# A hybrid GLA and SSD block on one core: own space for the split of h tiles 4 to 7, the scaled x of the SSD state taken from PSUM on VectorE, and the GLA output scaling shared by two engines

## The chip, the core and the metric

The kernel runs on one core of one Trainium2 chip. A core has TensorE (PE, matrix products, results in PSUM), VectorE (DVE), ScalarE (ACT), GpSimd (POOL) and SyncE (SP, which issues most DMAs). The metric is the device time of one execution in microseconds.

## The reference, cut to what matters

One layer on 2048 tokens of width 1024. The input projection feeds two token mixers; their outputs are concatenated, projected, and added to the input; a gated embedding follows.

```python
u = rmsnorm(h, norm_w)
q, k, v, g, gate_lr, z, xbc, dt_raw = split_columns(u @ w_in, SPLIT_SIZES)
# GLA: 4 heads, state 128 x 256
gla_out = rmsnorm(gla_chunked(q, k, v, log_a), gla_norm_w) * silu(g)
# SSD: 2 groups, 16 heads of 64, state 128
xs, bm, cm = split(silu(causal_depthwise_conv(xbc)))
def step(state, inp):                       # per chunk
    y = (cb * decay_ij) @ xdt + (ci @ state) * exp(cum)      # xdt = x * dt
    decay_to_end = exp(cum[-1] - cum)
    state = state * exp(cum[-1]) + bi^T @ (xdt * decay_to_end)
y = rmsnorm((y + xs * d_skip) * silu(z), ssd_norm_w)
h = h + concat(gla_out, y) @ w_out
gate = sigmoid(rmsnorm(h, pe_norm_w) @ w_pe_gate)
h = h + gate * (p_i @ w_pe)
out = rmsnorm(h, final_norm_w)
```

## The kernel before, in words

The tokens are worked on in four blocks of 512 (block 0 to 3), each of four steps of 128 tokens (t = 0 to 3). Activations lie with the channel on the partitions: a tile is 128 channels by 512 tokens. Every large product is made in three matmuls of split operands: each operand is a high half, rounded to the matmul's format, and a low half, the rest; TensorE adds high by high, high by low and low by high into one PSUM bank (`dense_t`, lines 254 to 256). Making the two halves of an activation is one ScalarE instruction for the high half, and one on VectorE or GpSimd for the low half. In block 0 the weights are split on the way (ScalarE L196, VectorE L197) and written back; blocks 1 to 3 load the split weights.

In each block the dense products of the input projection run on TensorE while the GLA heads and the SSD groups are worked on beside them. These side parts are Python generators, stepped in between the dense products; the order on each engine is then set by the framework's scheduler, so an engine's queue mixes instructions of several parts. PSUM has four banks for the dense products (`psd`) and four for the rest (`pss`). Each tile name has a few buffers; a new tile waits until the last reader of the buffer that it takes over is done.

The change touches four places.

The SSD steps (`ssd_steps`, two groups a block, four steps a group, so 32 steps). `make_x` transposes four tiles of x into a bank of PSUM (L602). VectorE multiplies the bank with `dt` to give `xd` (L604). GpSimd multiplies `xd` with `dte`, the decay to the end of the chunk, to give `xe` (L607). ScalarE casts `xe` to the high half of `xh` (L611), GpSimd makes the low half (L612). `make_m` makes the decay matrices `em` (two a step) from a DMA with ScalarE (L634, L636) and VectorE (L637). In the step proper TensorE makes `ips` (L652), `yps` from `xd` and `em` (L657), and `nps`, the new part of the state, from `xh` (L660 to L662). GpSimd decays the state `sS` (L663), VectorE adds (L665 to L670), where L665 makes `ec`, the part of the output that comes from the old state.

The end of a GLA head (`gla_steps`). The head's output stands in PSUM for four steps. ScalarE scales each step's 128x256 with the reciprocal norm `rs` (written in the profile as `yy`, after the chain L287 to L302 that makes it) to give `on` (L563). TensorE transposes `on` in two halves e2 = 0 and 1 (L569), VectorE multiplies with the gate (L573), ScalarE casts the high half into `mq` (L574) and GpSimd makes the low half (L575). Out-projection matmuls (L878 to L880) then read `mq`.

The h tiles. The last output projection of a block (`out_proj(ht, mqd, h_done)`) adds to the eight tiles of h (VectorE L881), and calls `h_done` for each tile d. This scales by the norm weight and splits: high half on ScalarE (L995), low half on VectorE (L996), squares on ScalarE (L350, L353) added up on GpSimd (L356). Tiles 0 to 3 go into one buffer of `mq`, tiles 4 to 7 into the next. There are two buffers, and one of them is `mqd`, which the projection itself reads until its end. The gate product then reads all eight (L254 to L256 with operand `mq`), and the sum of squares goes through TensorE (L320).

The table of `dte` (L472, L473), made once a block: 128 by four steps by 16 heads.

Of the kernel before, what the change touches and what calls it, by code (L numbers as in the profile page):

```python
# [6 lines left out]
F32 = mybir.dt.float32  # L7
F32R = mybir.dt.float32r
# [3 lines left out]
ALU = mybir.AluOpType  # L12
# [23 lines left out]
def hybrid_kernel(ctx, tc, x_nat, x_t, p_t, w_t, w_n0, w_n, w_o, w_g, w_p, prm, gup, cst, out):  # L36
# [384 lines left out]
    def lr_steps(lrn, lrT, dtr, cx):  # L421
# [51 lines left out]
        act(out=flat(dte), in_=flat(dte), func=AF.Exp)  # L473
        cx.update(dt=dt, cum=cum, elast=elast, dte=dte, cd=cd, ecd=ecd)
# [38 lines left out]
    def gla_steps(h, v, sg, fs, qm, km, mq):  # L513
# [48 lines left out]
        for t in range(NT):  # L562
            act(out=on[:, t, :], in_=rs_in[t // 2][:, (t % 2) * 256:(t % 2 + 1) * 256], func=AF.Copy,  # L563
                scale=rs[:, t:t + 1])
        yield
        for e2 in range(2):
            ps = pss.tile([P, TB], F32, name="pss")
            for t in range(NT):
# [6 lines left out]
            nc.gpsimd.tensor_tensor(out=mq[:, 1, kt, :], in0=og, in1=mq[:, 0, kt, :].bitcast(F32),  # L575
                                    op=ALU.subtract)
# [3 lines left out]
    def ssd_steps(g, bt, ctl, xs, cx):  # L580
# [18 lines left out]
        def make_x(t):  # L599
            xps = pss.tile([P, TB], F32, name="pss")  # L600
            for m in range(4):
                nc.tensor.transpose(out=xps[:, m * P:(m + 1) * P], in_=xs[:, m, t * P:(t + 1) * P], identity=ident)  # L602
            xd = sb.tile([P, 8, 64], F32, name="xd", tag="xd", bufs=SB["xd"])
            tt(out=xd, in0=xps.rearrange("p (h c) -> p h c", c=64),  # L604
               in1=dt[:, t, h8].unsqueeze(2).broadcast_to([P, 8, 64]), op=ALU.mult)
            xe = sb.tile([P, 8, 64], F32, name="xe", tag="tmp", bufs=SB["tmp"])
            nc.gpsimd.tensor_tensor(out=xe, in0=xd, in1=dte[:, t, h8].unsqueeze(2).broadcast_to([P, 8, 64]),  # L607
                                    op=ALU.mult)
# [101 lines left out]
    def new_mq():  # L710
        return big.tile([P, 2, 4, TB], F32R, name="mq", tag="mq", bufs=2)
# [41 lines left out]
    for b in range(NB):  # L753
# [232 lines left out]
        hw = [None, None]  # L986
        hsq = SumSq()

        def h_done(d):
            if d % 4 == 0:  # L990
                hw[d // 4] = new_mq()
            hd = ht[:, d, :]
            w = pr[:, C_PW + d:C_PW + d + 1]
            hq = hw[d // 4]
            act(out=hq[:, 0, d % 4, :], in_=hd, func=AF.Copy, scale=w)  # L995
            stt(out=hq[:, 1, d % 4, :], in0=hd, scalar=w, in1=hq[:, 0, d % 4, :].bitcast(F32),  # L996
                op0=ALU.mult, op1=ALU.subtract)
            hsq.add(hd)
# [14 lines left out]
        for d, cs in jobs:  # L1013
# [13 lines left out]
            gps = dense_t(lambda k: hw[k // 4][:, 0, k % 4, cs], lambda k: hw[k // 4][:, 1, k % 4, cs], n, gw[d],  # L1027
# [104 lines left out]
```

## Time and profile before

| | us |
|---|---|
| Runs | 1873.10, 1877.78, 1881.28 |
| Median | 1877.78 |
| The profiled execution | 1877.63 |
| Its span, first to last instruction | 1875.9 |
| TensorE busy | 1831.1 |
| VectorE busy | 1021.3 |
| ScalarE busy | 776.1 |
| GpSimd busy | 383.4 |

The mean granted clock of TensorE was 0.994 of full speed. Busy times are sums over the span; an instruction's time runs from its start to its end, and the ends of matmuls overlap the starts of the next. A wait is idle time of an engine just before an instruction; the profile names what ended it. Lines are those of the kernel before.

### The profile page before, as it was taken

The page shows a single profiled execution, that of the slowest core. Times are in us where ns is not written, and L with a number is a line of the kernel's source. Part 1 is how long each engine was busy: PE and PEld are TensorE (multiplying, and loading weights), DVE is VectorE, ACT ScalarE, POOL GpSimd, SP SyncE. Part 2 cuts the span into 40 slices and gives each one's busy share as a digit, 9 for nine tenths or more (in the row PEclk, how much of TensorE's full clock was granted, in tenths as well). Part 3 has the DMA queues.
Part 4 walks back from the last instruction along what each step waited for, and adds up shares of the span by engine and source line. Part 5 has one row for each costly group of instructions (what it writes and reads, how often), then busy time and mean ns, then how long its engine had stood idle before and what let it go on. Part 6 is the DMA issues. An engine that isn't in the chain of part 4 may idle for free.

```text
span 1875.9 us, 25880 instructions
## 1 busy us (share of the span) xinstructions
PE 1831.1 (98%) x9674; PEld 1538.6 (82%) x9674; DVE 1021.3 (54%) x1959; ACT 776.1 (41%) x1557; POOL 383.4 (20%) x355
## 2 busy tenths in 40 slices
PE   8989999999999999999999999999999999999997
PEld 6878888877887888887788788887888888888887
DVE  8776676477566345425555544523546545551544
ACT  6575454355355334224434533313424453321431
POOL 3132012034203101204311310301420221020222
PEclk9999999999999999999999999999999999999998
DMA  7767686778785557556568556655657755666651
GB/s 271 266 214 268 225 304 217 267 245 286 256 285 162 185 164 235 161 180 214 181 225 251 154 172 197 203 176 176 217 178 264 214 157 169 182 196 187 204 174 46
DMA packets 131853, 390.60 MB, mean 208 GB/s; under 512 B 13712, under 2 KB 32400, under 8 KB 131344
## 3 DMA queue, kind: packets, MB, share of 16 engines
q1 hardware_dynamic: 129744, 382.39, 63.0%
q0 software_dynamic: 1984, 6.55, 0.9%
q8 instruction: 76, 1.25, 0.3%
q14 instruction: 49, 0.40, 0.1%
HBM read 306.58 MB, written 82.31 MB: 207 GB/s over the span
## 4 chain that ended last, share of the span: by engine, by line
PE 76%; DVE 5%; DMA 4%; ACT 3%; issue 2%; POOL 1%; SPq 0%; DVEq 0%; ACTq 0%; POOLq 0%
PE psd L256 14%; PE psd L254 14%; PE psd L255 14%; PE psd L880 5%; PE psd L879 5%; PE psd L878 5%; PE psd L277 3%; PE psd L275 3%; PE psd L279 3%; PE pss L558 1%; PE pss L657 1%; PE pss L554 1%; DMA xp<-x_t 1%; PE pss L652 1%; DMA wkl<-wk_t 1%
## 5 line engine op out<-in xcount | busy, mean ns | idle before, releaser
L254 PE MATMUL psd<-u,wkl 128*128 128x512 f32 x864 | 343.0, 397 | 0.2
L255 PE MATMUL psd<-u,wkl 128*128 128x512 f32 x864 | 337.6, 391 | 0.0
L256 PE MATMUL psd<-u,wkl 128*128 128x512 f32 x864 | 337.2, 390 | 0.0
L254 PEld LDWEIGHTS psd<-u,wkl 128*128 128x128 f32 x864 | 162.3, 188 | 34.9 <-issue 1.9
L256 PEld LDWEIGHTS psd<-u,wkl 128*128 128x128 f32 x864 | 162.2, 188 | 34.1
L255 PEld LDWEIGHTS psd<-u,wkl 128*128 128x128 f32 x864 | 162.6, 188 | 32.5 <-issue 0.7
L356 POOL TENSOR_TENSOR sq<-sq,sqt 128x512 f32<-128x512 f32 (+1 forms) x77 | 98.7, 1282 | 396.5 <-ACT sqt L353 396.5
L879 PE MATMUL psd<-mq,wkl 128*128 128x512 f32 x384 | 151.5, 395 | 1.8 <-POOL mq L575 1.7
L878 PE MATMUL psd<-mq,wkl 128*128 128x512 f32 x384 | 153.2, 400 | 0.0
L412 DVE SCALAR_TENSOR_TENSOR acc<-psd,hcw,acc 128x511 f32<-128x511 f32 x144 | 107.1, 744 | 79.7 <-ACT acc L409 77.8
L880 PE MATMUL psd<-mq,wkl 128*128 128x512 f32 x384 | 150.0, 391 | 0.0
L197 DVE TENSOR_TENSOR whl<-wraw,whl 128x512 fp32r<-128x512 f32 (+1 forms) x136 | 110.1, 816 | 52.9 <-ACT whl L196 52.7
L881 DVE TENSOR_TENSOR ht<-ht,psd 128x512 f32<-128x512 f32 x128 | 87.3, 684 | 93.9 <-PE psd L880 93.2
L634 ACT ACTIVATE em<-em,cum 128x128 f32<-128x128 f32 x256 | 83.3, 391 | 105.2 <-DMA em<-cd 99.6
L196 ACT CAST whl<-wraw 128x512 fp32r<-128x512 f32 (+1 forms) x136 | 82.2, 618 | 72.2 <-PE psd L256 26.9
L275 PE MATMUL psd<-wkl,u 128*128 128x256 f32 (+1 forms) x384 | 111.5, 290 | 0.0
L277 PE MATMUL psd<-wkl,u 128*128 128x256 f32 (+1 forms) x384 | 109.8, 286 | 0.0
L279 PE MATMUL psd<-wkl,u 128*128 128x256 f32 (+1 forms) x384 | 109.7, 286 | 0.0
L254 PE MATMUL psd<-u,whl 128*128 128x512 f32 x272 | 108.9, 400 | 0.0
L255 PE MATMUL psd<-u,whl 128*128 128x512 f32 x272 | 107.6, 396 | 0.7 <-DVE u L389 0.4
L256 PE MATMUL psd<-u,whl 128*128 128x512 f32 x272 | 107.3, 395 | 0.3 <-DVE whl L197 0.3
L575 POOL TENSOR_TENSOR mq<-sg,mq 128x512 fp32r<-128x512 f32 x32 | 43.7, 1370 | 278.5 <-ACT mq L574 278.5
(282 smaller groups left out, 3940.0 us busy)
## 6 DMA issues: line engine op xcount, KB each, us to landing
wkl<-wk_t SPq DMA_DIRECT2D x216, 512.0 KB, 4.1
wkl<-wk_o SPq DMA_DIRECT2D x96, 512.0 KB, 3.6
wk_t<-whl SPq DMA_DIRECT2D x72, 512.0 KB, 3.7
wkl<-wk_g SPq DMA_DIRECT2D x44, 512.0 KB, 3.6
wraw<-w_t SPq DMA_DIRECT2D x36, 512.0 KB, 5.0
wkl<-wk_n SPq DMA_DIRECT2D x36, 512.0 KB, 3.6
em<-cd SPq DMA_DIRECT2D x64, 256.0 KB, 4.2
wk_o<-whl SPq DMA_DIRECT2D x32, 512.0 KB, 3.6
```

The costliest lines, as they stand in the source:

```text
L197: tt(out=t[:, 1, :], in0=s, in1=t[:, 0, :].bitcast(F32), op=ALU.subtract)
L254: mm(out=ps, lhsT=hi[:, sl], rhs=rhi(k), start=(k == 0), stop=False)
L255: mm(out=ps, lhsT=hi[:, sl], rhs=rlo(k), start=False, stop=False)
L256: mm(out=ps, lhsT=lo[:, sl], rhs=rhi(k), start=False, stop=(k == KT - 1))
L275: mm(out=outs[t], lhsT=ug(0, k)[:, ts], rhs=hi[:, sl], start=first, stop=False, skip_group_check=True)
L277: mm(out=outs[t], lhsT=ug(0, k)[:, ts], rhs=lo[:, sl], start=False, stop=False, skip_group_check=True)
L279: mm(out=outs[t], lhsT=ug(1, k)[:, ts], rhs=hi[:, sl], start=False, stop=last, skip_group_check=True)
L356: self.eng.tensor_tensor(out=self.acc[:, cs], in0=self.acc[:, cs], in1=sq, op=ALU.add)
L412: stt(out=acc[:, s:TB], in0=ps[:, 0:TB - s], scalar=w(j), in1=acc[:, s:TB], op0=ALU.mult, op1=ALU.add)
L878: mm(out=ps, lhsT=hi[:, sl], rhs=mq[:, 0, k, :], start=(k == 0), stop=False)
L879: mm(out=ps, lhsT=hi[:, sl], rhs=mq[:, 1, k, :], start=False, stop=False)
L880: mm(out=ps, lhsT=lo[:, sl], rhs=mq[:, 0, k, :], start=False, stop=(k == 3))
```

## The change

1. `dte` is multiplied by `dt` once a block, on VectorE.
2. In `make_x`, `xe` is made on VectorE from the PSUM bank with that product, ahead of `xd`; GpSimd has no part in it any more.
3. Of the four scalings of a GLA head's output the first two stay on ScalarE, the last two go to VectorE. Of the two low halves the second (e2 = 1) goes from GpSimd to VectorE.
4. Tiles 0 to 3 of h are split into a buffer of `mq` as before. Tiles 4 and 5 get a new tile `hx` in space of the name `xs`, tiles 6 and 7 get four tiles `hs` in spaces of `bt`, `ctl`, `cb` and `ec`, all names of the SSD part.

```diff
         act(out=flat(dte), in_=flat(dte), func=AF.Exp)
+        tt(out=dte, in0=dte, in1=dt, op=ALU.mult)
...
         for t in range(NT):
-            act(out=on[:, t, :], in_=rs_in[t // 2][:, (t % 2) * 256:(t % 2 + 1) * 256], func=AF.Copy,
-                scale=rs[:, t:t + 1])
+            o = rs_in[t // 2][:, (t % 2) * 256:(t % 2 + 1) * 256]
+            if t < 2:
+                act(out=on[:, t, :], in_=o, func=AF.Copy, scale=rs[:, t:t + 1])
+            else:
+                nc.vector.tensor_scalar_mul(out=on[:, t, :], in0=o, scalar1=rs[:, t:t + 1])
...
             nc.scalar.copy(out=mq[:, 0, kt, :], in_=og)
-            nc.gpsimd.tensor_tensor(out=mq[:, 1, kt, :], in0=og, in1=mq[:, 0, kt, :].bitcast(F32),
-                                    op=ALU.subtract)
+            eng = nc.vector if e2 else nc.gpsimd
+            eng.tensor_tensor(out=mq[:, 1, kt, :], in0=og, in1=mq[:, 0, kt, :].bitcast(F32), op=ALU.subtract)
...
+            xp3 = xps.rearrange("p (h c) -> p h c", c=64)
+            xe = sb.tile([P, 8, 64], F32, name="xe", tag="tmp", bufs=SB["tmp"])
+            tt(out=xe, in0=xp3, in1=dte[:, t, h8].unsqueeze(2).broadcast_to([P, 8, 64]), op=ALU.mult)
             xd = sb.tile([P, 8, 64], F32, name="xd", tag="xd", bufs=SB["xd"])
-            tt(out=xd, in0=xps.rearrange("p (h c) -> p h c", c=64),
-               in1=dt[:, t, h8].unsqueeze(2).broadcast_to([P, 8, 64]), op=ALU.mult)
-            xe = sb.tile([P, 8, 64], F32, name="xe", tag="tmp", bufs=SB["tmp"])
-            nc.gpsimd.tensor_tensor(out=xe, in0=xd, in1=dte[:, t, h8].unsqueeze(2).broadcast_to([P, 8, 64]),
-                                    op=ALU.mult)
+            tt(out=xd, in0=xp3, in1=dt[:, t, h8].unsqueeze(2).broadcast_to([P, 8, 64]), op=ALU.mult)
...
-        hw = [None, None]
+        hq = [None] * KT
...
+        def h_tiles(d):
+            if d == 0:
+                t = new_mq()
+                for k in range(4):
+                    hq[k] = (t[:, 0, k, :], t[:, 1, k, :])
+            elif d == 4:
+                t = sb.tile([P, 2, 2, TB], F32R, name="hx", tag="xs", bufs=SB["xs"])
+                for k in range(2):
+                    hq[4 + k] = (t[:, 0, k, :], t[:, 1, k, :])
+            elif d >= 6:
+                hq[d] = tuple(sb.tile([P, TB], F32R, name="hs", tag=tag, bufs=SB[tag])
+                              for tag in (("bt", "ctl"), ("cb", "ec"))[d - 6])
+
         def h_done(d):
-            if d % 4 == 0:
-                hw[d // 4] = new_mq()
+            h_tiles(d)
...
-            act(out=hq[:, 0, d % 4, :], in_=hd, func=AF.Copy, scale=w)
-            stt(out=hq[:, 1, d % 4, :], in0=hd, scalar=w, in1=hq[:, 0, d % 4, :].bitcast(F32),
-                op0=ALU.mult, op1=ALU.subtract)
+            hi, lo = hq[d]
+            act(out=hi, in_=hd, func=AF.Copy, scale=w)
+            stt(out=lo, in0=hd, scalar=w, in1=hi.bitcast(F32), op0=ALU.mult, op1=ALU.subtract)
```

The order on the engines changes with it. The first place is step t = 2 of the first SSD group in block 1, on TensorE. Before:

```order
L652 MATMUL pss<-ctl,sS_112 128x128 x4
L256 MATMUL psd<-u,wkl 128x512
L657 MATMUL pss<-em,xd 64x128 x3
L509 MATMUL pss<-v,kn 128x256
L510 MATMUL pss<-v,kn 128x256
L511 MATMUL pss<-v,kn 128x256
L657 MATMUL pss<-em,xd 64x128 x5
L254 MATMUL psd<-u,wkl 128x512
L660 MATMUL pss<-xh,bn 128x512
L255 MATMUL psd<-u,wkl 128x512
L661 MATMUL pss<-xh,bn 128x512
L662 MATMUL pss<-xh,bn 128x512
```

After, where the lines of the same code are three higher in this part (one higher in the GLA part):

```order
L256 MATMUL psd<-u,wkl 128x512
L254 MATMUL psd<-u,wkl 128x512
L255 MATMUL psd<-u,wkl 128x512
L256 MATMUL psd<-u,wkl 128x512
L660 MATMUL pss<-em,xd 64x128 x3
L510 MATMUL pss<-v,kn 128x256
L511 MATMUL pss<-v,kn 128x256
L512 MATMUL pss<-v,kn 128x256
L660 MATMUL pss<-em,xd 64x128 x5
L663 MATMUL pss<-xh,bn 128x512
L664 MATMUL pss<-xh,bn 128x512
L665 MATMUL pss<-xh,bn 128x512
```

A group of three dense matmuls (L254 to L256) has moved in front of the `em` matmuls (L657, now L660), and the three matmuls with `xh` (L660 to L662, now L663 to L665) stand together.

The same step on ScalarE, from the cast of the step before it to the cast of `xh` for this step. Before:

```order
L611 CAST xh<-xe 128x512
L636 ACTIVATE em<-em 128x512
L634 ACTIVATE em<-em,cum 128x128
L523 CAST amh<-am 128x512
L634 ACTIVATE em<-em,cum 128x128 x3
L543 ACTIVATE km<-gT_104,fs 128x256
L636 ACTIVATE em<-em 128x512
L634 ACTIVATE em<-em,cum 128x128 x5
L636 ACTIVATE em<-em 128x512
L611 CAST xh<-xe 128x512
```

After (`em` is L637 and L639 there, the cast L614):

```order
L614 CAST xh<-xe 128x512
L637 ACTIVATE em<-em,cum 128x128 x2
L524 CAST amh<-am 128x512
L639 ACTIVATE em<-em 128x512
L637 ACTIVATE em<-em,cum 128x128 x3
L544 ACTIVATE km<-gT_104,fs 128x256
L639 ACTIVATE em<-em 128x512
L637 ACTIVATE em<-em,cum 128x128 x4
L614 CAST xh<-xe 128x512
```

Between the two casts stood three exponentials of `em` (L636) before, and two after (L639).

The second place is the end of the last output projection in block 0, on ScalarE, where the h tiles are split. L196 splits weights, L387 makes the u of the next block. Before:

```order
L995 ACTIVATE mq<-ht,pr 128x512
L353 ACTIVATE sqt<-ht 128x512
L387 CAST u<-xp 128x512
L196 CAST wpe<-wraw 128x512 x2
L353 ACTIVATE sqt<-ht 128x512
L387 CAST u<-xp 128x512
L353 ACTIVATE sqt<-ht 128x512
L196 CAST whl<-wraw 128x512 x2
L353 ACTIVATE sqt<-ht 128x512
L387 CAST u<-xp 128x512
L995 ACTIVATE mq<-ht,pr 128x512 x4
L353 ACTIVATE sqt<-ht 128x512
```

After (the split is L1010):

```order
L353 ACTIVATE sqt<-ht 128x512
L196 CAST wpe<-wraw 128x512 x2
L1010 ACTIVATE hx<-ht,pr 128x512
L353 ACTIVATE sqt<-ht 128x512
L387 CAST u<-xp 128x512
L1010 ACTIVATE hx<-ht,pr 128x512
L353 ACTIVATE sqt<-ht 128x512
L196 CAST whl<-wraw 128x512 x2
L1010 ACTIVATE hs<-ht,pr 128x512
L353 ACTIVATE sqt<-ht 128x512
L387 CAST u<-xp 128x512
L1010 ACTIVATE hs<-ht,pr 128x512
```

The four splits of tiles 4 to 7, which stood together behind the projection, now stand each beside the square (L353) of its own tile.

## Rows read from the trace of the kernel before

**Rows 1.** Busy times and instructions by engine, whole span.

```profile
PE 1831.1 (98%) x9674; PEld 1538.6 (82%) x9674; DVE 1021.3 (54%) x1959; ACT 776.1 (41%) x1557; POOL 383.4 (20%) x355
```

**Rows 2.** TensorE's waits: line waited for, total us, times, longest us.

```profile
PE pss L661 <- POOL xh L612: 2.7, 4, 0.9
...
PE pss L660 <- ACT xh L611: 2.3, 4, 0.7
PE psd L879 <- POOL mq L575: 2.2, 4, 0.6
...
PE psd L254 <- ACT mq L995: 2.1, 1, 2.1
PE pss L660 <- DVE sh L290: 2.0, 1, 2.0
...
PE pss L657 <- DVE em L637: 1.8, 1, 1.8
PE pss L569 <- ACT on L563: 1.8, 3, 0.8
...
PE pss L320 <- POOL sq L356: 0.8, 2, 0.4
```

**Rows 3.** Windows: us; busy of PE, PEld, DVE, ACT, POOL; clock; DMA; GB/s.

```profile
95.00:105.00 10.00, 9.81 (x63) 8.16 (x64) 9.79 (x18) 8.00 (x21) 3.47 (x3) 1.00 0.96 288
111.90:115.30 3.40, 1.94 (x8) 0.98 (x7) 1.40 (x5) 1.97 (x5) 2.67 (x2) 1.00 1.00 276
115.40:118.70 3.30, 3.30 (x10) 2.71 (x11) 1.47 (x4) 1.75 (x5) 0.00 (x0) 0.50 0.85 339
129.10:132.40 3.30, 3.30 (x9) 2.58 (x8) 1.38 (x6) 0.13 (x1) 0.00 (x0) 0.50 0.67 266
```

**Rows 4.** Timeline of TensorE, block 1: start, us, operation, [idle before].

```profile
579.72 0.39 PE L255 MATMUL psd<-u,wkl 128*128 128x512 f32 x1
579.95 0.39 PE L256 MATMUL psd<-u,wkl 128*128 128x512 f32 x1
...
585.95 0.65 PE L657 MATMUL pss<-em,xd 128*64 128x128 f32 x6
...
588.95 0.50 PE L660 MATMUL pss<-xh,bn 128*128 128x512 f32 x1 [0.57 <-ACT xh L611]
...
602.16 0.33 PE L569 MATMUL pss<-cf,on 128*128 128x128 f32 x1 [0.48 <-ACT on L563]
```

**Rows 5.** Lines: busy us, mean ns; idle before, what ended it.

```profile
L604 DVE TENSOR_TENSOR xd<-pss,dt 128x512 f32<-128x512 f32 x32 | 21.9, 685 | 3.7 <-PE pss L602 3.7
...
L607 POOL TENSOR_TENSOR xe<-xd,dte 128x512 f32<-128x512 f32 x32 | 38.0, 1189 | 173.5 <-DVE xd L604 169.6 <-DVE fs L499 3.9
```

**Rows 6.** Timeline of VectorE, block 1, the crowded step.

```profile
584.80 0.69 DVE L604 TENSOR_TENSOR xd<-pss,dt 128x512 f32<-128x512 f32 x1
```

**Rows 7.** Timeline of GpSimd, blocks 0 and 1.

```profile
88.54 2.09 POOL L607 TENSOR_TENSOR xe<-xd,dte 128x512 f32<-128x512 f32 x1 [3.92 <-DVE fs L499]
...
586.87 1.04 POOL L607 TENSOR_TENSOR xe<-xd,dte 128x512 f32<-128x512 f32 x1
```

**Rows 8.** Timeline of TensorE, block 0, the SSD steps.

```profile
115.35 0.80 PE L661 MATMUL pss<-xh,bn 128*128 128x512 f32 x1 [0.85 <-POOL xh L612]
...
127.57 0.47 PE L660 MATMUL pss<-xh,bn 128*128 128x512 f32 x1 [2.04 <-DVE sh L290]
```

**Rows 9.** Timeline of VectorE, block 0, the SSD steps.

```profile
109.57 1.29 DVE L637 TENSOR_TENSOR em<-em,cb 128x512 f32<-128x512 f32 x2
...
121.49 2.13 DVE L637 TENSOR_TENSOR em<-em,cb 128x512 f32<-128x512 f32 x2
...
126.75 0.68 DVE L665 TENSOR_TENSOR ec<-ec,pss 128x512 f32<-128x512 f32 x1
```

**Rows 10.** Timeline of VectorE, block 0, split of the h tiles.

```profile
435.85 4.29 DVE L996 SCALAR_TENSOR_TENSOR mq<-ht,pr,mq 128x512 fp32r<-128x512 f32 x4 [0.71 <-ACT mq L995]
```

**Rows 11.** Timeline of TensorE, block 0, gate product.

```profile
439.65 2.08 PE L320 MATMUL pss<-sq,cf 128*128 128x512 f32 x2
```

More of the change, by code (lines that the diff above doesn't have):

```diff
@@ L985, in hybrid_kernel @@
             side.append(gu)
-        hw = [None, None]
+        hq = [None] * KT
         hsq = SumSq()
+        def h_tiles(d):
[10 more added lines that the diff above has]
+                              for tag in (("bt", "ctl"), ("cb", "ec"))[d - 6])
         def h_done(d):
-            if d % 4 == 0:
-                hw[d // 4] = new_mq()
+            h_tiles(d)
             hd = ht[:, d, :]
             w = pr[:, C_PW + d:C_PW + d + 1]
-            hq = hw[d // 4]
-            act(out=hq[:, 0, d % 4, :], in_=hd, func=AF.Copy, scale=w)
-            stt(out=hq[:, 1, d % 4, :], in0=hd, scalar=w, in1=hq[:, 0, d % 4, :].bitcast(F32),
-                op0=ALU.mult, op1=ALU.subtract)
+            hi, lo = hq[d]
+            act(out=hi, in_=hd, func=AF.Copy, scale=w)
+            stt(out=lo, in0=hd, scalar=w, in1=hi.bitcast(F32), op0=ALU.mult, op1=ALU.subtract)
             hsq.add(hd)
@@ L1026, in hybrid_kernel @@
                 mm(out=pps, lhsT=lo[:, sl], rhs=pb[:, ks], start=False, stop=(k == 1))
-            gps = dense_t(lambda k: hw[k // 4][:, 0, k % 4, cs], lambda k: hw[k // 4][:, 1, k % 4, cs], n, gw[d],
+            gps = dense_t(lambda k: hq[k][0][:, cs], lambda k: hq[k][1][:, cs], n, gw[d],
                           None if yh else h_sum)
```

## The prediction

> **What bounds the kernel now.** I read the busy times first [rows 1]: TensorE is busy 1831.1 us of a span of 1875.9, so at most some 45 us can be had without taking matmuls away, and this change takes none away. VectorE has 54%, ScalarE 41%, GpSimd 20%. So a move between those three counts only where TensorE waits for one of them. Next I read the table of TensorE's waits and kept the rows on lines that the change touches [rows 2]: the split state input `xh` (L660, L661), `em` (L657), the scaled GLA output (L569), the low half of the GLA output (L879) and the split of the h tiles (L254, L320). Then I followed each wait into the timelines, and read the granted clock around those in block 0 [rows 3]. The reader is to see that the waits are few and short. Together the rows of group 2 hold 15.7 us: under 1% of the span.
>
> A wait costs more than its idle time. A dense matmul that took 0.39 us was followed after 0.23 us by the next one [rows 4], so 0.16 us of overlap is lost with each wait.
>
> **The state input, xe from PSUM.** Before, `xd` is made on VectorE (32 of 685 ns), then GpSimd makes `xe` from it (32 of 1189 ns) [rows 5], then ScalarE the high half of `xh`, then GpSimd the low half. After, `xe` is the first VectorE operation on the PSUM tile and `xd` the second. In the crowded step of block 1, `xd` stood at 584.80 and took 0.69, and GpSimd began `xe` only at 586.87, behind other work of its own, and took 1.04 [rows 6, 7]. So `xe` ended at 587.91. With the change it ends at about 585.5: the chain to `xh` can win up to 2.4 us. How much it wins is set by ScalarE, which makes the high half in the order of its queue: the cast for this step moves ahead of one exponential (the order in the part on the change), about half a microsecond; the rest of what stands in front of it stays. TensorE waited there 0.57 us for the high half at 588.95 [rows 4], and for the low half, which GpSimd makes from it, again. In the whole run these are 2.3 + 2.7 us in four places each [rows 2], one in each block, and 8 x 0.16 us of lost overlap: 6.3 us. A whole dense group of three (3 x 0.23 = 0.69 us) also moves in front of the `em` matmuls in the new order of TensorE, which covers more. I take 5.0 of the 6.3 as gone, and leave 0.3 per block for the next late operand, `em` on ScalarE's queue. From the other side: nothing goes (0), or all does (6.3).
>
> In block 0 two more waits belong to this chain. At the first step `em` was 1.8 us late [rows 2]; ScalarE's `xh` cast stood in front of it, behind a GpSimd `xe` that began at 88.54 and took 2.09 [rows 7]. I take 1.0 of the 1.8. Then L660 waited 2.0 us at 127.57 [rows 2, 8]. The row names the tiny `sh`, but its bank was released by `ec`, which ended at 126.75 + 0.68 [rows 9]. `ec` stood behind an `em` pair that took 2.13 us beside GpSimd's `xe`, where the same pair took 1.29 at 109.57 [rows 9]. That saves 0.84, but `xe` itself comes in on VectorE with 0.69. What helps beyond the 0.15 is that the other GpSimd work moves out of the way. I take 1.1 of the 2.0; the ends are 0 and 2.0.
>
> On the difference between the two `em` pairs the Trainium skill has a rule (SBUF — State Buffer, "Who interferes with whom"): a VectorE instruction with two SBUF inputs contends with a GpSimd instruction that reads SBUF, one with at most one SBUF input does not. The two pairs here agree, 2.13 against 1.29 us. By it the new `xe` and `xd`, which read PSUM, never slow down, and 32 slowed neighbours go. The same skill (Perfetto Trace Analysis, "Optimizing Scalar/DVE Operations") warns that moving work between GpSimd and VectorE might not help, since they share a read port. For the PSUM reads the first rule excludes that here; for the low halves of the GLA output, two SBUF inputs, it would hold, and then that edit is worth nothing, as the sum nearly has it.
>
> **The clock.** In block 0 the granted clock was 0.50 in two stretches of 3.3 us in which TensorE was busy all the time; the first came directly behind a stretch in which it was busy 1.94 of 3.40 us, with these very waits in it [rows 3, 8]. At full clock each stretch is half as long: 1.65 us each, 3.3 together. I take all of the first and half of the second, 2.5, because half of the wait ahead of the second remains; ends 0 and 3.3.
>
> **The h split.** Before, tiles 4 to 7 went into the second buffer of `mq`, which is free only when the last output projection has read it, so four high and four low halves came in a bunch: VectorE took 4.29 us for the four lows [rows 10]. The wait at L254 for it is 2.1 us, at block 0 only; blocks 1 and 2 lose 0.8 at the sum of squares L320 [rows 2]. After, each is split as its h tile is made. In block 0 I expect no gain: VectorE has its weight splits and h additions between the lows, so the last low comes hardly sooner, and the sum of squares that L320 takes in at 439.65 [rows 11] still comes through GpSimd's additions. In blocks 1 and 2 the wait on the squares goes: 0.8 + 2 x 0.16 = 1.1. Ends: 0, and with block 0 2.1 + 0.16 more. The new space (`xs`, `bt`, `ctl`, `cb`, `ec`) is free there, since the SSD steps of the block are done; if one were still held, the split would wait as it did before.
>
> **The GLA output.** Of 64 scalings 32 go from ScalarE to VectorE, of 32 low halves 16 go from GpSimd to VectorE. L569 waited 1.8 us [rows 2], but for the *first* `on`, which stays on ScalarE: at 602.16 a single transpose waits [rows 4]. I take 0 (ends 0 and 1.8). L879 waits for the first low half of the last head, which stays on GpSimd: 2.2 in four places [rows 2], of which 0.4 may go because the operations in front come sooner (ends 0 and 2.2).
>
> **What it adds.** VectorE gets 32 x 0.685 = 21.9 us of `xe`, and 32 scalings and 16 low halves, which no row of VectorE shows; by the row of `xd` they are at most 48 x 0.685 = 32.9 us, all beside TensorE's work at the end of a head, where it waits for the first scaling only. Where it has slack this costs nothing: the cover is TensorE's own work. The bank of the transposed x is held some 0.69 us longer, and `xd` is later by as much. In the crowded step `xd` ended at 585.49 and TensorE came to it at 585.95 [rows 4, 6], 0.46 us of slack, so alone it would be 0.23 us late; with the 0.69 us of dense work placed in front, the slack is 0.46 again. Where VectorE is full, 9.79 of 10 us at 95 to 105 [rows 3], some shows. I put +1.0 for all of it (ends 0 and 21.9). The product of `dte` and `dt`, four tiny operations on 128x64, costs nothing: it is done long before the steps.
>
> **Sum.** -5.0 - 1.0 - 1.1 - 2.5 - 1.1 - 0.4 + 1.0 = -10.1 us, against the profiled execution's 1877.63 (1.7 us around its span, 0.15 below the median shown): 1867.5 us.
>
> **Rivals.**
> 1. *The waits only move on.* Of the 6.3 us 2 go, because `em` or `ec` is late instead, the clock dips stay, and the additions cost 1.0: 1876.6, with 1873 to 1879 around it. For it speaks that ScalarE's and VectorE's queues are crowded in just these steps; against it that a group of dense matmuls moved in front. Chance 0.27.
> 2. *All goes.* 6.3 + 1.8 + 2.0 + 2 x 0.16 + 3.3 + 1.1 + 2.3 for block 0's split + 2.2 for L879 = 19.3, with nothing added: 1858.3, or 1854 to 1862. For it speaks that the covers are large in the other steps; against it that block 0's split has a second chain behind it. Chance 0.15.
> 3. *Slower: VectorE becomes the bound of the SSD steps.* `xd` is behind `xe`, and L657 waits for `xd` at each step: up to 32 x 0.685 = 21.9 us, less gains of 11.1 at most: 1888.4. It decides if the slack before L657 is under 0.69 us in most steps; 0.46 in the crowded step and 9.79 of 10 busy speak for it, against it that VectorE was busy only 54% of the span [rows 1] and that three steps in four have dense groups between the transposes and L657. Chance 0.08.
>
> **Numbers.** The forecast has 0.50, with 1862 to 1873 as its own range. No change within 0.5% (9.4 us, about what a measurement of this kernel can tell) is 1868.4 to 1887.2. Of the forecast's 0.50 I put 0.29 below 1868.4; with rival 2 that is 0.44 faster. Rival 1 and the rest of the forecast are 0.48, rival 3 is 0.08. The range 1856 to 1879 leaves out most of rival 3 and the lower end of rival 2.
>
> **What would show it.** Right: `xe` is on VectorE at some 685 ns; the rows L660 and L661 for `xh` (new L663, L664) are gone or below 0.3 us each; the half-clock stretch at 115 us is gone; the L320 waits at blocks 1 and 2 are gone; VectorE about 25 us busier, GpSimd 38 less for `xe`. Wrong: new waits at the `em` matmuls for `xd`, or at the transposes of x for their bank; a longer wait at L569 because VectorE is late with its two scalings; or block 0's gate stage losing its 2.1 us after all.

## The result, and the profile after

Four runs of the changed kernel took 1861.55 to 1866.62 us, median 1866.01; the kernel before had a median of 1879.51 beside them. The ratio is 0.9923, with a 95% interval of 0.9904 to 0.9942. Measured again on another chip it was 0.9919 (0.9896 to 0.9942). The profiled execution has a span of 1864.8 us, 11.1 less than before.

The busy times of the changed kernel answer to [rows 1]:

```profile
PE 1823.6 (98%) x9674; PEld 1538.5 (82%) x9674; DVE 1053.0 (56%) x2043; ACT 763.2 (41%) x1525; POOL 325.6 (17%) x307
```

VectorE is 32 us busier, GpSimd 58 us less busy; TensorE's instructions are the same in number.

TensorE's waits in the changed kernel answer to [rows 2] (line waited for, total us, times, longest):

```profile
PE pss L573 <- ACT on L566: 3.3, 3, 1.8
PE pss L320 <- POOL sq L356: 3.0, 2, 2.7
...
PE pss L660 <- DVE em L640: 2.5, 3, 1.8
...
PE psd L882 <- POOL mq L580: 2.2, 4, 0.6
...
PE psd L254 <- ACT whl L196: 1.5, 1, 1.5
...
PE psd L1038 <- DVE gth L1047: 1.4, 1, 1.4
PE pss L518 <- DVE ec L668: 1.3, 2, 0.6
```

The two rows for `xh` (5.0 us), the 2.0 at L660, and the 2.1 for `mq` at L254 have no row any more. The wait for `on` has grown from 1.8 to 3.3; the low half of the last GLA head is where it was, 2.2; the sum of squares has grown from 0.8 to 3.0 (2.7 of it in block 0, where the kernel before had no such wait, and 0.3 in block 2), and waits for the weight split and the gate stand in block 0.

Where the 11.1 us of the profile came from is read from the starts of the sum-of-squares matmuls (L320), which end the stages of both kernels. "Start" runs up to the first of these places, "first SSD group" from the first to the second; "gate" is the last output projection of block 0 with the gate product behind it. The table gives, for the changed kernel and each experiment told below, what the stage gained on the same stage before, in us of the profiled execution. The last column is the time lost to half clock in the first 520 us, read from the granted clock in windows of half a microsecond (6.8 us before; the run's last microseconds are at half clock in every kernel and are left out).

| Kernel | start | block 0, first SSD group | block 0, to the last projection | block 0, gate | block 1 | block 2 | block 3 | sum | at half clock |
|---|---|---|---|---|---|---|---|---|---|
| changed | -1.8 | 5.7 | 2.4 | 0.6 | 0.1 | 2.6 | 1.5 | 11.1 | 3.4 |
| the same again | 0.0 | 7.4 | 3.0 | 0.6 | -0.9 | 3.4 | 1.3 | 14.7 | 1.7 |
| xe_only | -1.7 | 6.2 | 3.1 | -0.8 | -0.1 | 2.0 | -0.3 | 8.3 | 1.7 |
| xe_sbuf | -1.6 | 5.1 | 2.8 | -0.9 | -0.7 | 1.3 | 0.5 | 6.6 | 5.1 |
| gla_only | 0.0 | 2.9 | 1.7 | 0.1 | -1.4 | 0.7 | -0.9 | 3.1 | 1.7 |
| h_only | 0.2 | 0.0 | -1.7 | -1.7 | 0.2 | 1.7 | -1.9 | -3.1 | 8.5 |
| no_h | -0.1 | 6.3 | 3.8 | 0.6 | -1.3 | 0.5 | 0.8 | 10.7 | 1.7 |
| xe_twice | -1.8 | 5.9 | 2.4 | 0.5 | 1.2 | 2.0 | -0.9 | 9.3 | 3.4 |
| on_dve | 0.2 | 7.4 | 3.4 | 0.3 | 0.6 | 3.5 | 3.0 | 18.4 | 1.7 |
| on_dve_again | 0.4 | 6.7 | 3.7 | 0.8 | 2.1 | 4.1 | 1.3 | 19.1 | 1.7 |
| on_lo_dve | -0.2 | 6.7 | 4.6 | 0.6 | 2.1 | 4.3 | 3.5 | 21.7 | 1.7 |
| late_u | -0.5 | 6.8 | 2.5 | 0.4 | 0.8 | 2.3 | 1.8 | 14.1 | 3.4 |

Two profiles of the same changed kernel differ by 3.7 us, 1.7 of it half clock; a difference of a microsecond or two in one cell is within that. The half clock moves time between cells too: the kernel before lost 3.4 us in the first SSD group and 3.4 in the gate stage of block 0, the changed kernel 1.7 in the start and 1.7 on the way to the last projection. Three quarters of the gain in the first profile lie in block 0, before its gate stage.

The windows of the changed kernel (columns as in [rows 3]): full clock at the place of the stretch at 115 us, and a half-clock stretch that was not there before.

```profile
117.30:120.60 3.30, 3.30 (x21) 2.86 (x21) 2.28 (x8) 2.66 (x7) 0.00 (x0) 1.00 0.58 209
...
186.70:188.90 2.20, 2.20 (x7) 1.71 (x6) 2.09 (x6) 1.18 (x3) 0.00 (x0) 0.50 0.00 0
```

In 3.3 us 21 matmuls now, where 10 went through before.

**The crowded step.** The timeline of the changed kernel at the step of [rows 4, 6, 7] (engines one after the other):

```profile
578.00 0.68 DVE L609 TENSOR_TENSOR xe<-pss,dte 128x512 f32<-128x512 f32 x1
578.60 0.68 DVE L611 TENSOR_TENSOR xd<-pss,dt 128x512 f32<-128x512 f32 x1
...
579.08 1.28 ACT L637 ACTIVATE em<-em,cum 128x128 f32<-128x128 f32 x4 [5.16 <-DMA em<-cd]
580.27 0.60 ACT L614 CAST xh<-xe 128x512 fp32r<-128x512 f32 x1
...
580.95 1.28 POOL L615 TENSOR_TENSOR xh<-xe,xh 128x512 fp32r<-128x512 f32 x1 [0.85 <-ACT xh L614]
...
579.84 0.65 PE L660 MATMUL pss<-em,xd 128*64 128x128 f32 x6
...
581.76 0.50 PE L663 MATMUL pss<-xh,bn 128*128 128x512 f32 x1
582.28 0.50 PE L664 MATMUL pss<-xh,bn 128*128 128x512 f32 x1
```

`xe` is ready at 578.7, but the cast begins at 580.27: ScalarE stands at four `em` operations that waited for a DMA until 579.08. The high half is ready at 580.87 and TensorE comes to it at 581.76, with the extra dense group behind it; the low half is ready at 582.23, just in time. `xd` ends at 579.28, before TensorE comes to it at 579.84, a slack of 0.56 us where 0.46 was reckoned.

**The scaled GLA output.** The same kernel, end of that head:

```profile
593.84 0.88 DVE L568 TENSOR_SCALAR on<-pss,yy 128x256 f32<-128x256 f32 x2
...
593.60 1.28 ACT L637 ACTIVATE em<-em,cum 128x128 f32<-128x128 f32 x4 [3.34 <-DMA em<-cd]
595.75 0.40 ACT L637 ACTIVATE em<-em,cum 128x128 f32<-128x128 f32 x1 [0.86 <-DMA em<-cd]
596.05 0.82 ACT L566 ACTIVATE on<-pss,yy 128x256 f32<-128x256 f32 x2
...
596.56 0.44 PE L573 MATMUL pss<-cf,on 128*128 128x128 f32 x2 [1.80 <-ACT on L566]
```

VectorE's two scalings are done at 594.7. ScalarE's two begin at 596.05: in its queue stands an `em` operation whose DMA has not come. TensorE waits 1.8 us for data whose inputs had been there since 593.8.

**The gate stage of block 0.** Here three waits stand in the place of the old one: those for the weight split (1.5) and the gate (1.4) in the list above, and the longest, for the sum of squares:

```profile
429.24 0.67 DVE L884 TENSOR_TENSOR ht<-ht,psd 128x512 f32<-128x512 f32 x1
...
430.05 1.27 POOL L389 TENSOR_TENSOR u<-xp,u 128x512 fp32r<-128x512 f32 x1 [1.94 <-ACT u L387]
431.33 1.66 POOL L356 TENSOR_TENSOR sq<-sq,sqt 128x512 f32<-128x512 f32 x1
...
433.04 1.12 PE L320 MATMUL pss<-sq,cf 128*128 128x512 f32 x2 [2.70 <-POOL sq L356]
```

The projection's last matmuls began before 422, but VectorE adds the last h tile only at 429.24; its square goes through GpSimd behind a `u` tile and ends at 432.99, and L320 starts then.

### The profile page after: what moved, and what is told of

Read it like the earlier page. It is cut to its first block, busy times and chain, and to the rows that moved or that the text cites. A ratio compares the mean times of both kernels' runs of the same rounds, so it can differ in the third digit from the quotient of the medians.

```text
span 1864.8 us, 25875 instructions
## 1 busy us (share of the span) xinstructions
PE 1823.6 (98%) x9674; PEld 1538.5 (82%) x9674; DVE 1053.0 (56%) x2043; ACT 763.2 (41%) x1525; POOL 325.6 (17%) x307
## 4 chain that ended last, share of the span: by engine, by line
PE 79%; DMA 3%; DVE 3%; issue 2%; ACT 2%; POOL 1%; SPq 0%; DVEq 0%; ACTq 0%; POOLq 0%
PE psd L254 14%; PE psd L256 14%; PE psd L255 14%; PE psd L882 5%; PE psd L883 5%; PE psd L881 5%; PE psd L277 3%; PE psd L275 3%; PE psd L279 3%; DMA em<-cd 1%; PE pss L660 1%; PE pss L559 1%; PE pss L655 1%; PE pss L555 1%; PE pss L320 1%
## 5 line engine op out<-in xcount | busy, mean ns | idle before, releaser
L254 PE MATMUL psd<-u,wkl 128*128 128x512 f32 x864 | 342.1, 396 | 0.0
L256 PE MATMUL psd<-u,wkl 128*128 128x512 f32 x864 | 337.5, 391 | 0.0
L256 PEld LDWEIGHTS psd<-u,wkl 128*128 128x128 f32 x864 | 162.2, 188 | 33.9
L254 PEld LDWEIGHTS psd<-u,wkl 128*128 128x128 f32 x864 | 162.3, 188 | 33.2 <-issue 1.4
L637 ACT ACTIVATE em<-em,cum 128x128 f32<-128x128 f32 x256 | 83.3, 391 | 116.1 <-DMA em<-cd 115.9
L197 DVE TENSOR_TENSOR whl<-wraw,whl 128x512 fp32r<-128x512 f32 (+1 forms) x136 | 101.6, 754 | 48.0 <-ACT whl L196 47.6
L196 ACT CAST whl<-wraw 128x512 fp32r<-128x512 f32 (+1 forms) x136 | 81.9, 617 | 79.7 <-PE psd L256 22.5
L254 PE MATMUL psd<-u,whl 128*128 128x512 f32 x272 | 107.7, 396 | 0.0
L256 PE MATMUL psd<-u,whl 128*128 128x512 f32 x272 | 106.3, 391 | 0.3 <-DVE whl L197 0.3
L882 PEld LDWEIGHTS psd<-mq,wkl 128*128 128x128 f32 x384 | 72.2, 188 | 17.7 <-POOL mq L580 3.0
```

What stands on the lines that cost most here:

```text
L197: tt(out=t[:, 1, :], in0=s, in1=t[:, 0, :].bitcast(F32), op=ALU.subtract)
L254: mm(out=ps, lhsT=hi[:, sl], rhs=rhi(k), start=(k == 0), stop=False)
L256: mm(out=ps, lhsT=lo[:, sl], rhs=rhi(k), start=False, stop=(k == KT - 1))
L882: mm(out=ps, lhsT=hi[:, sl], rhs=mq[:, 1, k, :], start=False, stop=False)
```

## The experiments

The theory: `xe` on GpSimd, and its place in the queues, cost nearly all that was won; GLA and h edits are worth little by themselves. The first rival: the three edits share the gain. Three runs have one edit each, with the lines as in the diff above.

**xe_only**: the new `dte`, and `xe` ahead of `xd` on VectorE.

```diff
+        tt(out=dte, in0=dte, in1=dt, op=ALU.mult)
...
+            tt(out=xe, in0=xp3, in1=dte[:, t, h8].unsqueeze(2).broadcast_to([P, 8, 64]), op=ALU.mult)
...
-            nc.gpsimd.tensor_tensor(out=xe, in0=xd, in1=dte[:, t, h8].unsqueeze(2).broadcast_to([P, 8, 64]),
```

> Only xe from PSUM on VectorE (with the product of dte and dt); GLA scaling and h split as before. Theory (the gain is the chain to xh and what hangs on it): 9 to 11 us of the 13 are kept, ratio to before 0.994 to 0.995; L660/L661 waits for xh under 0.5 us in all, no half-clock stretch at 115 us, the ec waits of block 0's second group (1.4 and 1.0 us) gone too; the gate stage of block 0 keeps its 2.1 + 0.8 us for mq and its half clock behind it. Rival (the three edits share the gain): 3 to 6 us, ratio 0.997 to 0.998.

Measured: 1870.41 against 1878.61, ratio 0.9955 (0.9941 to 0.9968): 8.4 us, a little short of the 9 to 11 of the theory, well above the rival's 3 to 6. The wait for `xh` is 0.3 us in all; the wait on `mq` is back at 2.1 (and 0.8 behind it). Its row of TensorE's waits for `xh`:

```profile
PE pss L661 <- POOL xh L612: 0.3, 1, 0.3
```

The half clock behind it was expected too, and was not there. The waits for `ec` in block 0's second group are gone, as expected. Of what is missing from the 9 to 11 us, the waits for `on` hold some: they are 3.0 us in this run, 1.2 more than before, though all four scalings are still on ScalarE. The rest is not accounted for.

**gla_only**: the two scalings and one low half on VectorE.

```diff
+                nc.vector.tensor_scalar_mul(out=on[:, t, :], in0=o, scalar1=rs[:, t:t + 1])
...
+            eng = nc.vector if e2 else nc.gpsimd
```

> Only the GLA edits: two of four scalings and one of two low halves on VectorE. Theory (TensorE waits for the first scaling, which stays on ScalarE behind em operations that wait for a DMA): 0, within 2 us of before; the waits for on stay at 1.8 us or grow, those for the low half on GpSimd stay at 2.2 us. Rival (shorter scaling chain helps): waits for on under 1 us, 2 to 3 us faster, ratio 0.9985.

Measured: 1877.56 against 1878.61, ratio 1.0000 (0.9990 to 1.0011). No gain, as the theory had it; the wait for `on` 2.0. This run tells something else. Its waits for `xh` in block 0 are those of before, but the clock behind them stays full. Its timeline there:

```profile
114.14 0.50 PE L663 MATMUL pss<-xh,bn 128*128 128x512 f32 x1 [0.66 <-ACT xh L614]
115.50 0.50 PE L664 MATMUL pss<-xh,bn 128*128 128x512 f32 x1 [0.86 <-POOL xh L615]
```

and the window behind it, columns as in [rows 3]:

```profile
115.50:118.80 3.30, 3.30 (x20) 2.91 (x21) 1.80 (x5) 2.42 (x6) 0.00 (x0) 1.00 0.85 334
```

So the same waits, at the same place, are followed by half clock in one profile (before, and h_only) and not in another.

**h_only**: the h split alone (`h_tiles` and the new `h_done`).

> Only the own space for h tiles 4 to 7. Theory: 1 to 3 us, ratio 0.9985 to 0.9995: the wait on mq (2.1 + 0.8 us) and the half clock behind it in block 0 go, but waits for the weight split (about 2 us) and for the sum of squares (about 2.7 us) stand in their place; blocks 1 and 2 lose their 0.4 us each. Rival (the split was the bound of the gate stage): 5 us or more, ratio 0.997, with no wait at L320 above 1 us.

Measured: 1879.13 against 1878.61, ratio 1.0002 (0.9993 to 1.0010); neither the 1 to 3 us of the theory nor the rival's 5. Of the waits expected in block 0, that for the weight split came, that for the squares didn't, and another did (TensorE's waits of h_only):

```profile
PE psd L1035 <- DVE gth L1044: 2.6, 1, 2.6
...
PE psd L254 <- ACT whl L196: 1.5, 1, 1.5
```

These hold 4.1 us of TensorE's time, where 2.1 + 0.8 went. In blocks 1 and 2 the stretch from the last output projection to the end of the gate product became 0.9 and 1.0 us shorter (104.0 us before in each). In this profile 8.5 us are lost to half clock, so its sum is no measure of the edit.

Next: does it matter that `xe` reads PSUM, or only that GpSimd doesn't make it? And does VectorE pay for it?

**xe_sbuf**: `xe` on VectorE from `xd`, behind it, else as before.

```diff
-            nc.gpsimd.tensor_tensor(out=xe, in0=xd, in1=dte[:, t, h8].unsqueeze(2).broadcast_to([P, 8, 64]),
-                                    op=ALU.mult)
+            tt(out=xe, in0=xd, in1=dte[:, t, h8].unsqueeze(2).broadcast_to([P, 8, 64]), op=ALU.mult)
```

> xe on VectorE, but as in the kernel before from xd in SBUF (behind xd); nothing else changed. Theory (the gain is that GpSimd's slow operation, and its place in GpSimd's queue, leave the chain to xh; PSUM as the source is not the point): within 3 us of xe_only, ratio to before 0.995 to 0.997. Rival (PSUM as the source is what pays, since an operation with two SBUF operands is slowed beside GpSimd): xe above 0.8 us in the mean, ratio 0.998 to 1.0.

Measured: 1870.48 against 1878.11, ratio 0.9951 (0.9937 to 0.9966), the same as xe_only. The line of `xe` in it:

```profile
L607 DVE TENSOR_TENSOR xe<-xd,dte 128x512 f32<-128x512 f32 x32 | 22.0, 687 | 0.4
```

and the wait for the low half of `xh` that stays, in TensorE's waits:

```profile
PE pss L660 <- POOL xh L611: 3.5, 4, 1.0
```

687 ns with two operands in SBUF, 685 from PSUM: the source is not the point in this kernel, where 28 of the 32 `xe` met no GpSimd operation. The Trainium skill (Perfetto Trace Analysis, "Optimizing Scalar/DVE Operations") warns that work moved between GpSimd and VectorE might not help, since they share a read port; here 1189 ns became 687, and with 0.9951 it did help. The four waits of the low half all lie in blocks 1 to 3, and hold as much there as the waits for `xh` did before. In xe_only TensorE waits in those blocks for `on` instead, 3.0 us in three places, where xe_sbuf has none. So in blocks 1 to 3 the waits mostly moved on to the next late operand, and the gain of both runs is mostly in block 0: here 5.1 us in the first SSD group and 2.8 in the rest.

**no_h**: xe and GLA as in the changed kernel, h split as before.

> As the changed kernel, but the h tiles split as before (second buffer of mq). Theory (the h split alone was worth nothing in time): the same as the changed kernel within 2 us, ratio 0.992 to 0.994; in block 0 the waits on mq of 2.1 + 0.8 us are back and those for the sum of squares (2.7) go below 1.2. Rival (the h split carries the gap between xe_only, 0.9955, and the changed kernel, 0.9923): ratio 0.995 to 0.996.

Measured: 1867.27 against 1878.11, ratio 0.9937 (0.9923 to 0.9951). It lies in the theory's range (0.992 to 0.994), within the interval of the changed kernel and just outside that of xe_only; a contribution of the h split of up to some 2 us is not excluded by the times. In block 0 the wait on `mq` is back and none for the sum of squares is left, as expected; the two waits of the second row are those of blocks 1 (0.9) and 2 (0.4) (TensorE's waits of no_h):

```profile
PE psd L254 <- ACT mq L998: 2.1, 1, 2.1
...
PE pss L320 <- POOL sq L356: 1.3, 2, 0.9
```

Its gate stage in block 0 gains as much as that of the changed kernel, 0.6, with 1.7 us lost to half clock in it, where the changed kernel lost none.

**xe_twice**: the changed kernel with a second, idle `xe` in front of `xd`.

```diff
             tt(out=xe, in0=xp3, in1=dte[:, t, h8].unsqueeze(2).broadcast_to([P, 8, 64]), op=ALU.mult)
+            tt(out=xe, in0=xp3, in1=dte[:, t, h8].unsqueeze(2).broadcast_to([P, 8, 64]), op=ALU.mult)
```

> As the changed kernel, with xe written twice in a row from PSUM: 32 more VectorE operations of about 0.685 us (21.9 us), in front of xd, which holds the bank longer by as much. Theory (VectorE has slack before the em matmuls in most steps): 0 to 5 us slower than the changed kernel, ratio to before 0.992 to 0.995. Rival (VectorE is the bound of the SSD steps): 15 to 22 us slower, ratio 1.000 to 1.004.

Measured: 1868.60 against 1878.11, ratio 0.9943 (0.9926 to 0.9960). The line of the second `xe`:

```profile
L610 DVE TENSOR_TENSOR xe<-pss,dte 128x512 f32<-128x512 f32 x32 | 21.9, 685 | 0.3
```

21.9 us of work added, some 2 to 4.5 us paid: the lower figure by the times (1868.60 against the 1866.01 and 1866.27 of the changed kernel), the higher by the ratios (0.9943 against 0.9923 and 0.9919); the intervals overlap. VectorE is not the bound of the SSD steps.

**on_dve**: the changed kernel with all four scalings on VectorE, after the reading of the 1.8-us wait above.

```diff
-            if t < 2:
-                act(out=on[:, t, :], in_=o, func=AF.Copy, scale=rs[:, t:t + 1])
-            else:
-                nc.vector.tensor_scalar_mul(out=on[:, t, :], in0=o, scalar1=rs[:, t:t + 1])
+            nc.vector.tensor_scalar_mul(out=on[:, t, :], in0=o, scalar1=rs[:, t:t + 1])
```

> As the changed kernel, but all four scalings of a GLA head on VectorE. Theory (in the changed kernel the two on VectorE are ready 2 us before the two on ScalarE, which stand behind em operations that wait for a DMA): the 3.3 us of waits for on are gone, 3 to 4 us faster than the changed kernel, about 1862 where that is 1866, ratio to before 0.990 to 0.991. Rival (the wait is the norm's chain on VectorE): waits for on stay above 2 us, time as the changed kernel, ratio 0.992 to 0.993.

Measured: 1861.65 against 1878.61, ratio 0.9915 (0.9899 to 0.9930). No wait for `on` is left. The changed kernel did not run beside it, so both were measured again on one chip:

> The changed kernel once more, to be compared with the next two on the same chip: 0.992 to 0.993 of the kernel before. The waits of its profile as in the first one (on 3.3 us in three places, low half 2.2 in four); half-clock stretches may lie elsewhere.

> All four scalings of a GLA head on VectorE, once more. Theory (the two scalings on ScalarE stood behind em operations that wait for a DMA): 3 to 4 us under the changed kernel of this comparison, no wait for on. Rival (the two are the same, what was seen was the half-clock stretches): within 1.5 us of it.

Measured: the changed kernel 1866.27 (six runs, 1862.09 to 1869.33), on_dve 1859.69 (six runs, 1858.08 to 1861.24); every run of the second is under every run of the first. 6.6 us between the medians, more than the 3 to 4 of the theory; its profile has no wait for `on`. Those waits, 3.3 us and 3 x 0.16 of lost overlap, are 3.8 of the 6.6; the rest is not explained. Against the kernel before, on_dve had 0.9915 the first time and 0.9884 the second, the changed kernel 0.9923 and 0.9919, so 6.6 may be on the high side.

**on_lo_dve**: as on_dve, and both low halves of the last head on VectorE.

```diff
-            eng = nc.vector if e2 else nc.gpsimd
+            eng = nc.vector if e2 or h == 3 else nc.gpsimd
```

> As on_dve, and both low halves of the last head on VectorE. Theory (the low half is late because GpSimd takes 1.5 us for it where VectorE takes about 0.7): the four waits of 0.56 us at the first low half go, 2 us under on_dve. Rival (VectorE's queue at that place is as late as GpSimd): the wait stays, now for VectorE, same time as on_dve.

Measured: 1857.48 (1854.65 to 1859.00), ratio to before 0.9870 (0.9851 to 0.9890), 2.2 us under on_dve, as expected; the two sets of runs overlap by 0.9 us. The four waits of 0.56 are gone. The low halves on either engine, in its lines:

```profile
L577 DVE TENSOR_TENSOR mq<-sg,mq 128x512 fp32r<-128x512 f32 x20 | 13.4, 689 | 6.4 <-ACT mq L575 6.2
...
L577 POOL TENSOR_TENSOR mq<-sg,mq 128x512 fp32r<-128x512 f32 x12 | 15.5, 1292 | 215.1 <-ACT mq L575 215.1
```

This is the fastest version found, 8.8 us under the changed kernel on the same chip.

**late_u**: on_dve, and in block 0 the u tiles of block 1 made behind the last output projection.

```diff
+            if b:
+                side.append(gu)
...
         out_proj(ht, mqd, h_done)
+        if b == 0:
+            side.append(gu)
...
+            if b == 0 and d >= 1:
+                step()
```

> As on_dve (all four scalings on VectorE), and in block 0 the u tiles of block 1 are made behind the last output projection instead of beside it. Theory (VectorE and GpSimd, full of weight splits and u tiles beside that projection, make the h tiles and their squares late): the waits of block 0's gate stage (1.6 + 1.0 for the weight split, 1.1 to 2.7 for the squares, 1.5 at the gate) fall by 3 us or more, ratio to before 0.989 to 0.990. Rival (only the place moves, and the u tiles are late for block 1): same as on_dve or slower, ratio 0.9915 or more, with waits for u at L255 in block 1.

Measured: 1863.56 against 1878.11, ratio 0.9913 (0.9898 to 0.9929): the rival's number, but not its sign, since block 1 has no wait for u. The stage moved its waits (timeline of TensorE in late_u):

```profile
426.55 0.70 PE L320 MATMUL pss<-sq,cf 128*128 128x512 f32 x1 [1.41 <-POOL sq L356]
...
452.14 0.50 PE L254 MATMUL psd<-mq,whl 128*128 128x512 f32 x1 [0.81 <-ACT whl L196]
...
454.34 0.80 PE L256 MATMUL psd<-mq,whl 128*128 128x512 f32 x1 [1.47 <-DVE whl L197]
```

In on_dve, which it edits, the wait for the squares was 1.1 us and those for the weight split 1.6 + 0.7, earlier in the stage. So the squares came no sooner, the waits for the weight split only moved, and the theory is not borne out.

## Why the prediction was right, point by point

1867.5 was forecast, 1866.01 measured. The sum held; its terms did not all, and that it came within 1.5 us is partly luck: the waits for `on` went the wrong way, the term for `em` came in one profile of two, and a gain of over 2 us that no term foresaw made up for them. Of the signs of being right, `xe` at 685 ns, the rows for `xh` and the half clock at 115 us came as said; a wait at L320 was left, 0.3 in block 2 in one profile and 0.9 in block 1 in the other.

- **The state input, 5.0.** The waits at L660 and L661 did go. But in blocks 1 to 3, where 3.5 of the 5.0 lay, they mostly moved on, as the first rival has it: all waits of TensorE there add up to 14.0 us before and 12.8 after. xe_sbuf kept 3.5 us of waits for `xh` and had the same time as xe_only, and in the changed kernel block 1 gained only 0.1, since its wait for `on` grew by 1.3. The gain of all stages of blocks 1 to 3 together is 4.1 us, with the h split in it; in the second profile it is 3.8. "How much it wins is set by ScalarE" was right: the cast waits for ScalarE's `em` operations, now by 1.6 us behind its data.
- **em at the first step, 1.0 of 1.8.** This step failed in its mechanism: the wait is 1.82 as before, and what ends it is not what was reckoned. The timeline of the kernel before there:

```profile
93.83 1.22 DVE L637 TENSOR_TENSOR em<-em,cb 128x512 f32<-128x512 f32 x1 [4.04 <-ACT em L636]
...
93.46 1.04 POOL L663 TENSOR_TENSOR sS<-sS,elast 128x512 f32<-128x512 f32 x1 [0.81 <-PE pss L652]
```

  of the changed kernel:

```profile
92.28 1.28 DVE L500 TENSOR_TENSOR fs<-gD,b 128x4 f32<-128x4 f32 x1
...
95.81 1.11 DVE L640 TENSOR_TENSOR em<-em,cb 128x512 f32<-128x512 f32 x1 [1.52 <-ACT em L639]
...
91.83 1.71 POOL L615 TENSOR_TENSOR xh<-xe,xh 128x512 fp32r<-128x512 f32 x1 [4.44 <-ACT xh L614]
95.33 1.04 POOL L666 TENSOR_TENSOR sS<-sS,elast 128x512 f32<-128x512 f32 x1 [1.79 <-PE pss L655]
...
97.06 0.66 PE L660 MATMUL pss<-em,xd 128*64 128x128 f32 x8 [1.82 <-DVE em L640]
```

  and of its second profile:

```profile
93.19 0.69 DVE L640 TENSOR_TENSOR em<-em,cb 128x512 f32<-128x512 f32 x1 [1.52 <-ACT em L639]
...
93.45 1.34 POOL L666 TENSOR_TENSOR sS<-sS,elast 128x512 f32<-128x512 f32 x1 [2.53 <-PE pss L655]
...
94.03 0.66 PE L660 MATMUL pss<-em,xd 128*64 128x128 f32 x8 [0.66 <-DVE em L640]
```

  GpSimd decays the state `sS` as soon as TensorE has read it (L652, now L655). In the first two timelines VectorE's `em` begins while that decay runs, and ends 0.55 us behind it (95.05 after 94.50, 96.92 after 96.37). So the wait has the same size, however early the chain in front of `em` was: it is 1.82 in nine of the thirteen profiles, and 1.90 in one in which `em` began just before the decay's end. In the other three, the one above, xe_twice and on_dve, `em` began first, took 0.69 us, and TensorE waited 0.66 to 0.71. The prediction looked at the cast in front of `em`, not at the decay beside it. In the changed kernel `em` was also held up by `fs`, a VectorE operation of 128x4 elements which took 1.28 us beside GpSimd's low half (median of its sixteen: 0.155), but that doesn't decide: in the second profile `fs` took 1.28 as well. The Trainium skill (SBUF — State Buffer, "Who interferes with whom") has a VectorE operation with two SBUF inputs contend with a GpSimd operation that reads SBUF; these rows agree, and xe_sbuf shows the other side, 687 ns in the mean where 28 of the 32 operations met no GpSimd operation. That the slowed neighbours of GpSimd's `xe` would go, as the prediction says, didn't come: `em` took 785 ns in the mean before and 847 after, since other GpSimd operations, the low half of `xh` and the decay, now meet it.
- **ec at 127.57, 1.1 of 2.0.** All of it went, 0.9 more than reckoned.
- **The clock, 2.5.** Both stretches of the first SSD group are gone, 3.4 us. With the waits there, 6.1 us before and 3.3 after, that makes up the 5.7 us which the group gained, within 0.5. gla_only shows the clock alone: it had the waits (6.1) and full clock, and gained 2.9 there. But the changed kernel lost 3.4 us in two other places, and one profile is a weak measure. Each run has a mean granted clock, and its shortfall from 1, times the span, is the time lost at half clock, with the run's end in it: 10.4 us in the mean of 43 runs of the kernel before, 7.3 in ten of the changed kernel, 8.2 in xe_only and 7.8 in xe_sbuf, but 11.6 in gla_only and 11.4 in h_only. So some 3 us of the gain are the clock's, they come with `xe` on VectorE, and the size of this term was right. Which wait brings the half clock on stays open, since the same waits were followed by it in one profile and not in another.
- **The h split, 1.1.** From the last output projection to the end of the gate product, blocks 1 and 2 gain 1.1 and 0.4, 1.5 together. All eight profiles with the split gain there, 1.0 to 2.4 us together, and the four without it between -0.3 and 0.1; so this term is borne out by the traces, too small to show in the times. Block 0 gains 0.6 in its gate stage, as no_h does without the split. But two things moved in it against each other: before, the stage lost 3.4 us to half clock (436.2 to 443.0 us), for which the prediction had no term, and in the changed kernel it lost none; TensorE's waits in it grew from 3.5 to 6.4 us. No gain by the split is seen there, as forecast, and the timeline above puts the longest wait down to the squares, which go through GpSimd.
- **The GLA output, 0 + 0.4.** This step failed: `on` lost 1.5 us instead of 0, at the half that stayed on ScalarE. The loss came with `xe`, not with the GLA edit: xe_only has 3.0 us of these waits with all four scalings on ScalarE, gla_only 2.0. The low half stayed at 2.2.
- **What it adds, 1.0.** A second `xe`, 21.9 us of work, cost some 2 to 4.5 us (xe_twice), so this size was fair or somewhat low; what the first cost is not seen by itself.
- **Not foreseen:** 2.4 to 4.6 us in the rest of block 0, in every kernel with `xe` on VectorE, and 1.7 in gla_only. Two waits for `ec`, of 1.4 and 1.0 us at L517 and L509, account for most of it. The timeline of the kernel before at the first of them:

```profile
288.31 0.75 DVE L637 TENSOR_TENSOR em<-em,cb 128x512 f32<-128x512 f32 x1 [2.10 <-ACT em L636]
...
289.70 0.82 DVE L197 TENSOR_TENSOR whl<-wraw,whl 128x512 fp32r<-128x512 f32 x1
290.43 0.68 DVE L665 TENSOR_TENSOR ec<-ec,pss 128x512 f32<-128x512 f32 x1
...
291.16 0.60 PE L517 MATMUL pss<-qm,km 128*128 128x128 f32 x3 [1.43 <-DVE ec L665]
```

  and of the changed kernel:

```profile
285.57 0.68 DVE L668 TENSOR_TENSOR ec<-ec,pss 128x512 f32<-128x512 f32 x1
286.17 0.68 DVE L640 TENSOR_TENSOR em<-em,cb 128x512 f32<-128x512 f32 x1
...
286.70 0.72 PE L518 MATMUL pss<-qm,km 128*128 128x128 f32 x5
```

  `ec` frees the bank that L517 (now L518) takes. Before, it stood on VectorE behind an `em` operation, for which VectorE sat idle 2.10 us, and behind a weight split; in the new order it stands ahead of `em`, and TensorE goes on without a wait. So the timelines put this gain down to the scheduler's new order and not to the operation itself, and it fits that in gla_only, where `xe` did not move, the first of the two waits is 0.55. No run changes the order alone, so this cause is not shown.

What stays open: why half clock fell behind the waits of the first SSD group in some profiles and not in others; what made up the rest of the 6.6 us by which on_dve was faster; and whether the h split's 1.5 us show in the times (no_h 0.9937, changed kernel 0.9923 and 0.9919, with overlapping intervals).

## What to carry to other kernels

When an engine works its queue in order, an operation that TensorE waits for should not share a queue with operations that wait for DMAs: sharing the scalings between two engines gained nothing by itself, moving the rest of them off ScalarE gained 6.6 us between the medians of six runs each. An operation in the middle of a chain of four engines is worth moving to an engine with half its time free even if that engine is the busier one: 21.9 us more on VectorE bought 8.4 us of time, and another 21.9 cost 2 to 4.5. Where a wait keeps its size though the chain in front of it got shorter, look for what runs beside its last operation: here GpSimd's decay beside `em`. And when a sum comes out right, its terms should still be measured one by one: here `em` came in one profile of two, `on` went the wrong way, and a gain of over 2 us was in none of them.

## What the runs showed of the hardware that was not expected

The same waits of TensorE (0.66 and 0.86 us at 114 to 115.5) were followed by 3.4 us at half clock in one profile and by full clock in another. Two profiles of one kernel lay 3.7 us apart. A VectorE operation of 128x4 elements took 1.28 us beside a GpSimd operation, against a median of 0.155. In the trace of the changed kernel 16 of the 64 `em` operations on VectorE (median 0.69 us) began while a GpSimd operation with two inputs ran, and every one of them ended 0.55 us behind it; where `em` began first, at the first step of three other profiles, it took 0.69 us and GpSimd's decay 1.34 to 1.38 instead of 1.04.
